# Scale sums at first use, seven banks for the MLP's products, three single-block groups at each end, a last norm by halves and square sums on GpSimd

## The chip, the cores and the metric

The program runs on one core of a Trainium2 chip, in one launch. The metric is its device time in microseconds; of the runs shown the median counts. The profile is of one execution by itself. PE is TensorE, DVE is VectorE, ACT is ScalarE, POOL is GpSimd, and SP is the engine that issues most transfers.

## The reference

One decoder layer on 2048 tokens of width 1024, in float32 throughout; h is the normed x of the line above:

```python
mem_n = rmsnorm(mem, mem_norm_g)                    # 256 memory tokens
q, k, v, g, u = split(rmsnorm(x) @ w_in)            # 512 columns each
y_ret = silu(g) * head_rmsnorm(retention(rope(q), rope(k), v))   # 4 heads
y_pool = pool_mixer(u, pool_w) * pool_scale         # windows 2, 4, 8, 16
x = x + concat(y_ret, y_pool) @ w_out
x = x + softmax((h @ wq) @ (mem_n @ wk).T / 16) @ (mem_n @ wv) @ wo   # 4 heads
a = h @ w_up                                        # 5632 columns
c = conv_w[0]*a[t-2] + conv_w[1]*a[t-1] + conv_w[2]*a[t] + conv_b
x = x + (silu(c[:, :2816]) * c[:, 2816:]) @ w_down
return rmsnorm(x, final_norm_g)
```

## The kernel before

The activations lie transposed: a tile holds 128 features by 512 tokens. The 2048 tokens are two blocks (b = 0, 1) of 1024, each with two halves (s = 0, 1). Every large product is a form with seven multiplications (i = 0 to 6) in place of eight: the weight of a pair of output tiles is four quarters, of which seven sums are made (`make(i)`), and the tokens are made into seven sums likewise. Each sum is cut into a high and a low fp16 part by `cut` (L274 on ACT for the high part, L241 or L232 on DVE for the low one), and `passes` multiplies high by high, high by low and low by high (L289, L290, L291). So one of the seven products of one block is 12 matmuls of 128x128 by 128x512 for an up group, and a group of one block is 84.

Before a weight is cut it is scaled by a power of two. `fetch` loads its four quarters, ACT squares each (L250), and `power` adds the four sums on DVE (L260), adds them over the partitions by a one-column matmul on PE (L264, into a bank of the ring called side) and makes the scale from the exponent (L236, L238). The cut needs that scale.

What sets the order: the program is written in one line of Python, in which `step` mixes side work (generators, put in with `beside(gen, rate)`) into the products at a rate per product, and a scheduler then orders the instructions of each engine, earlier code first where several are ready. The order within an engine is fixed when the kernel runs. PSUM has eight banks, handed out in rings: for the MLP six are for the products (mm) and two for the small matmuls (side).

The stages:

- 0 to about 150 us: `folded_weights` multiplies the memory into the attention's weights and W_o, `x_block` squares the tokens of block 0 and norms them, and the rope tables are made. `stats` adds squares over the features by matmuls against a column of ones (L315), DVE makes the reciprocal root in eleven small operations, and `spread` puts the result on all partitions: a diagonal matrix by DVE (L232), then a matmul against ones (L328).
- 150 to about 1213: input projections, retention, pooling, output projection and cross-attention.
- 1213 to 2070: the up products. `Up` groups f = 0 to 21 give a pair of gate and value tiles, with convolution (`conv`) on ACT (L1217), DVE and, for sums, POOL. The first EARLY groups and the last LATE run for block 0 alone and then, with their cut weights read back from WUd, for block 1 alone; the others run for both blocks at once. While the first round runs, `mlp_tokens(1)` norms, sums and cuts the tokens of block 1. While the fourth runs, `down_weights` cuts the down weights and writes them to WDd.
- 2070 to 2531: the down products (`Down`), three parts of four groups for each block, with weights read from WDd (L1127) and tokens read from Gd. After the last part of block 0 its final norm runs beside the products of block 1.
- 2531 to 2554: the final norm of block 1, over both halves, and its outputs (L1354, L1361).

`run` makes weight sums ahead of the product that needs them, up to seven products ahead (AHEAD). `squares` (ACT squares, another engine adds) takes the engine of the add as its argument. The names in the listings: mm, aux and side are PSUM banks; G and FD are the pools of SBUF tiles; rn and rnm hold norms, sm small results, sb sums, scl_t scales, taps the scaled convolution weights.

## Time and the profile before

| | us |
|---|---|
| three runs | 2557.42, 2563.1, 2565.51 |
| median | 2563.1 |
| the profiled execution | 2555.96 |
| its span on the core | 2554.2 |
| PE busy | 2386.9 (93%) |
| DVE busy | 1689.4 (66%) |
| ACT busy | 1221.1 (48%) |
| POOL busy | 567.7 (22%) |

A row of the windows gives, for a stretch of the span, its length, then the busy time and the number of instructions of PE, of PE's weight loads, of DVE, ACT and POOL, then the clock granted to PE, the share of the DMA engines and GB/s. A row of waits reads: engine, what it was to write and its line, what released it; then the waiting time in all, how often, and the longest. A row of the timeline starts with the time from the span's start and the duration; behind the shapes stands how many instructions it groups and, in brackets, how long the engine had been idle and what ended that. A busy PE is not a PE at its peak, because the matmuls overlap: their starts are what counts.

### The profile page before, as it was taken

How to read it: one execution, taken by the hardware profiler on the slowest of the kernel's cores; microseconds unless marked ns; L12 is line 12 of the kernel's file. 1: busy time of each engine (PE TensorE's matmuls, PEld its weight loads, DVE VectorE, ACT ScalarE, POOL GpSimd, SP SyncE). 2: the span in 40 equal slices, each digit the busy share in tenths (PEclk: the TensorE clock that was granted, in tenths of full speed). 3: DMA queues.
4: the chain of work that ended last, by engine and by line, in shares of the span. 5: the costliest groups of instructions: out<-in, count | busy, mean ns of one | idle time of the engine just before them, and what ended most of it. 6: DMA issues, size and time to landing. Idle time of an engine off the chain costs nothing. (4 is left out here: it accounts for less than half of the span.)

```text
span 2554.2 us, 32142 instructions
## 1 busy us (share of the span) xinstructions
PE 2386.9 (93%) x11461; PEld 1178.6 (46%) x11461; DVE 1689.4 (66%) x2852; ACT 1221.1 (48%) x2343; POOL 567.7 (22%) x372
## 2 busy tenths in 40 slices
PE   7799999999999999999799999898999998998997
PEld 7645554465444454444344444343444443444443
DVE  8834888455656462671968786776776786766764
ACT  6763345322643242252467666665765564244322
POOL 0000112011222101312613232432322133323210
PEclk9899999999999999999899999999999999999998
DMA  7671224100443023023233323333323454655751
GB/s 259 201 232 46 75 66 137 37 26 13 158 151 119 34 91 108 33 87 106 86 111 115 101 88 106 116 112 108 120 95 103 161 183 164 206 182 181 239 182 66
DMA packets 177040, 306.67 MB, mean 120 GB/s; under 512 B 18416, under 2 KB 49264, under 8 KB 176880
## 3 DMA queue, kind: packets, MB, share of 16 engines
q1 hardware_dynamic: 175728, 302.52, 35.8%
q8 instruction: 90, 1.47, 0.2%
q10 hardware_dynamic: 1152, 2.10, 0.2%
q14 instruction: 70, 0.57, 0.1%
HBM read 212.53 MB, written 92.01 MB: 119 GB/s over the span
## 5 line engine op out<-in xcount | busy, mean ns | idle before, releaser
L289 PE MATMUL mm<-G 128*128 128x512 f16 x1955 | 744.6, 384 | 57.1 <-DVE FD L232 12.1
L290 PE MATMUL mm<-G 128*128 128x512 f16 x1955 | 749.5, 383 | 2.9 <-DVE G L232 2.5
L291 PE MATMUL mm<-G 128*128 128x512 f16 x1955 | 740.6, 383 | 3.4 <-DVE G L241 2.1
L232 POOL TENSOR_TENSOR G<-G 128x512 f32<-128x512 f32 (+5 forms) x261 | 386.6, 1486 | 1577.8 <-DVE G L241 658.4
L290 PEld LDWEIGHTS <-G 128*128 128x128 f16 x2848 | 280.6, 99 | 368.3 <-issue 53.7
L289 PEld LDWEIGHTS <-G 128*128 128x128 f16 x2848 | 281.1, 99 | 367.0 <-issue 29.0
L291 PEld LDWEIGHTS <-G 128*128 128x128 f16 x2848 | 280.7, 99 | 351.6 <-issue 16.9
L241 DVE SCALAR_TENSOR_TENSOR G<-G,scl_t 128x512 f16<-128x512 f32 (+2 forms) x416 | 343.8, 850 | 141.5 <-ACT G L274 130.3
L274 ACT ACTIVATE G<-G,scl_t 128x512 f16<-128x512 f32 x352 | 244.0, 713 | 307.5 <-POOL G L232 99.6
L241 DVE SCALAR_TENSOR_TENSOR G<-mm,scl_t,G 128x512 f32<-128x512 f32 (+1 forms) x279 | 207.6, 747 | 246.8 <-PE mm L291 228.3
L289 PE MATMUL mm<-FD,G 128*128 128x512 f16 x893 | 340.4, 383 | 3.1 <-ACT G L274 2.3
L291 PE MATMUL mm<-FD,G 128*128 128x512 f16 x893 | 339.8, 381 | 2.5 <-DVE G L241 2.5
L290 PE MATMUL mm<-FD,G 128*128 128x512 f16 x893 | 340.5, 381 | 0.0
L241 DVE SCALAR_TENSOR_TENSOR FD<-FD,taps 128x1024 f32<-128x1024 f32 (+2 forms) x162 | 234.8, 1469 | 37.5 <-ACT FD L1217 36.5
L232 DVE TENSOR_TENSOR G<-G 128x512 f32<-128x512 f32 (+4 forms) x274 | 215.8, 813 | 50.0 <-ACT G L350 17.5
L350 ACT ACTIVATE G<-G 128x512 f32<-128x512 f32 x108 | 67.4, 627 | 204.6 <-DVE G L241 186.3
L250 ACT ACTIVATE G<-G 128x512 f32<-128x512 f32 x136 | 84.9, 625 | 109.1 <-DVE G L241 70.0
L289 PE MATMUL mm<-G,FD 128*128 128x512 f16 x327 | 124.7, 383 | 4.0 <-ACT FD L1191 3.2
L289 PE MATMUL mm<-FD 128*128 128x256 f32 (+2 forms) x313 | 106.9, 344 | 21.3 <-ACT FD L447 7.2
L290 PE MATMUL mm<-G,FD 128*128 128x512 f16 x327 | 124.6, 381 | 0.0
L291 PE MATMUL mm<-G,FD 128*128 128x512 f16 x327 | 124.3, 381 | 0.1
L1217 ACT ACTIVATE FD<-FD,vecs,taps 128x1024 f32<-128x1024 f32 x81 | 99.4, 1235 | 38.1 <-DVE FD L232 37.2
(169 smaller groups left out, 2600.8 us busy)
## 6 DMA issues: line engine op xcount, KB each, us to landing
G<-WDd SPq DMA_DIRECT2D x112, 256.0 KB, 3.5
Gd<-FD SPq DMA_DIRECT2D x41, 512.0 KB, 2.8
G<-xT SPq DMA_DIRECT2D x80, 256.0 KB, 3.3
G<-Gd SPq DMA_DIRECT2D x67, 256.0 KB, 3.6
G<-w_qkgu SPq DMA_DIRECT2D x64, 256.0 KB, 2.9
FD<-w_up SPq DMA_DIRECT2D x45, 256.0 KB, 3.0
G<-w_up SPq DMA_DIRECT2D x43, 256.0 KB, 3.1
G<-WDd SPq DMA_DIRECT2D x56, 192.0 KB, 3.0
```

Of the source, the lines that this page charges most:

```text
L232: return eng.tensor_tensor(out=out, in0=a, in1=b, op=op)
L241: dve.scalar_tensor_tensor(out=out, in0=a, scalar=s, in1=b, op0=op0, op1=op1)
L250: act.activation(junk.f[:, : src.shape[-1]], src, AF.Square, accum_out=col)
L274: act.activation(hi, src, AF.Identity, scale=scale)
L289: pe.matmul(ps, lh, rh, start=start, stop=False, skip_group_check=more)
L290: pe.matmul(ps, lh, rl, start=False, stop=False, skip_group_check=more)
L291: pe.matmul(ps, ll, rh, start=False, stop=stop, skip_group_check=more)
L350: act.activation(q.f, src, AF.Square)
L1217: act.activation(c.f, a[:, at : at + T], AF.Identity, bias=cb[:, f : f + 1], scale=tap[2])
```

## The change

- `Member.fetch` only loads and squares; the scale sum (`power`) moves into `weigh`, which the first `make` of the weight calls.
- The MLP's rings are seven banks for products and one for small matmuls.
- EARLY and LATE go from 2 to 3: three groups at each end run one block at a time, sixteen instead of eighteen run for both. The cut up weights written to WUd and read back go from 28 to 42.
- At the start of the MLP fifteen weight sums are made ahead (FIRST), later up to seven products ahead, and in the down products ten.
- `down_weights` has two more pauses after each fetch and runs at 0.52 steps a product instead of 0.42.
- `spread` is split into `diagonals` and `spread`, with pauses between in `tokens_norm`. The memory norm becomes a generator, and three projections instead of two are begun around its parts.
- The fourteen adds of the token squares of block 0 go from DVE to POOL; half of the evacuations of the W_o product go from DVE to ACT.
- The last norm runs by halves: that of half 1 is written as soon as its last sum exists, that of half 0 after the last product, and then the outputs of the one and of the other. The final norm of block 0 runs at twice its rate.

```diff
-EARLY, LATE = 2, 2
+EARLY, LATE = 3, 3
-AHEAD = 7
+FIRST, AHEAD, AHEAD_DOWN = 14, 7, 10
...
-    def spread(y):
+    def diagonals(y, d=None):
         n = y.shape[1]
-        d = S.take()
-        w = d.f[:, : n * P]
-        tt(dve, w.rearrange("p (a b) -> p a b", a=n), ident.rearrange("p (o b) -> p o b", o=1).to_broadcast([P, n, P]), bcast(y, P), ALU.mult)
-        ps = bank("side")[:, : n * P]
+        d = d or S.take()
+        tt(dve, d.f[:, : n * P].rearrange("p (a b) -> p a b", a=n), ident.rearrange("p (o b) -> p o b", o=1).to_broadcast([P, n, P]), bcast(y, P), ALU.mult)
+        return d, n * P
+    def spread(d):
+        d, n = d
+        ps = bank("side")[:, :n]
+        pe.matmul(ps, ones, d.f[:, :n], start=True, stop=True)
         d.free()
         return ps
...
         yield
+        yield
+        ds = [diagonals(y[:, 4 * s : 4 * s + 4]) for s in range(NS)]
+        yield
+        yield
         for s in range(NS):
-            ps = spread(y[:, 4 * s : 4 * s + 4])
+            ps = spread(ds[s])
             r = S.take()
...
+            yield
             dve.tensor_copy(rn, stats([s_m.f[:, :NMEM]]))
-            act.activation(rm.f[:, :NMEM], spread(rn), AF.Copy)
             s_m.free()
+            d = diagonals(rn)
+            yield
+            act.activation(rm.f[:, :NMEM], spread(d), AF.Copy)
...
-        begun = [project(0, first), project(1)]
-        memory_norm()
+        begun = [project(0, first)]
+        norm = memory_norm()
+        next(norm)
+        begun.append(project(1))
+        next(norm)
+        begun.append(project(2))
+        next(norm, None)
         for n in range(KT):
-            ps = begun[n] if n < 2 else project(n)
+            ps = begun[n] if n < 3 else project(n)
...
                     t, at = S.take(), 4 * h + 2 * mt + nh
-                    ts(dve, t.f, ps, rn[:, mt : mt + 1], ALU.mult)
+                    if nh:
+                        act.activation(t.f, ps, AF.Identity, scale=rn[:, mt : mt + 1])
+                    else:
+                        ts(dve, t.f, ps, rn[:, mt : mt + 1], ALU.mult)
...
-                squares(k, x.f, acc[s].f, dve)
+                squares(k, x.f, acc[s].f, pool if b == 0 else dve)
...
             if self.source is not None:
                 self.raw = True
-                self.up, self.inv = scales[self.key]
                 return
             if self.key not in scales:
-                c = counts(4)
+                self.sums = counts(4)
                 for i, r in enumerate(self.raw.values()):
-                    squared(r.f[:, :w], c[:, i : i + 1])
-                scales[self.key] = power(c, TOP4)
+                    squared(r.f[:, :w], self.sums[:, i : i + 1])
+
+        def weigh(self):
+            if self.key not in scales:
+                scales[self.key] = power(self.sums, TOP4)
             self.up, self.inv = scales[self.key]
         def make(self, i):
             w = self.n * P
+            if i == 0:
+                self.weigh()
...
+            if i == 0 and self.j == KT // 2 - 1 and b + 1 == NB:
+                spare.extend(S.take() for _ in range(4))
             if i in (3, 4, 5):
                 pending.append(lambda: self.out({3: 0, 4: 3, 5: 1}[i]))
+                if i == 5 and self.j == KT // 2 - 1 and b + 1 == NB:
+                    while pending:
+                        pending.pop(0)()
+                    self.half = self.norm_half(1)
             elif i == 6:
                 if self.j == KT // 2 - 1:
                     while pending:
                         pending.pop(0)()
                     self.out(2)
-                    self.norm()
+                    if b + 1 == NB:
+                        late = self.norm_half(0)
+                        self.last_outputs(*self.half)
+                        self.last_outputs(*late)
+                    else:
+                        self.norm()
                 else:
                     pending.append(lambda: self.out(2))
...
-                beside(steps(), 0.5)
-                return
-            y = stats([r.f for r in done])
-            for s in range(NS):
-                ps = spread(y[:, 4 * s : 4 * s + 4])
-                r = S.take()
-                act.activation(r.f, ps, AF.Copy)
+            def steps():
+                yield from tokens_norm(done, rb)
-                    v = Y[b, n // 2, n % 2 * 2 + s].f
-                    if n % 3 == 2:
-                        tt(pool, v, v, r.f, ALU.mult)
-                    else:
-                        tt(dve, v, v, ps, ALU.mult)
-                    (act if n % 2 else sp).dma_start(outputs(n, s), v)
+            beside(steps(), 1.0)
+
+        def norm_half(self, s):
+
+            ps = spread(diagonals(stats([sums[s].f]), spare.pop()))
+            r = spare.pop()
+            act.activation(r.f, ps, AF.Copy)
+            return s, ps, r
+
+        def last_outputs(self, s, ps, r):
+            for n in range(KT):
+                v = Y[self.b, n // 2, n % 2 * 2 + s].f
+                if n % 3 == 2:
+                    tt(pool, v, v, r.f, ALU.mult)
+                else:
+                    tt(dve, v, v, ps, ALU.mult)
+                (act if n % 2 else sp).dma_start(self.outputs(n, s), v)
...
-            while made < len(items) and made <= at + AHEAD:
+            while made < len(items) and made <= max(at + (AHEAD_DOWN if isinstance(m, Down) else AHEAD), FIRST):
...
-    rings.update(mm=[0, 1, 2, 3, 4, 5], side=[6, 7])
+    rings.update(mm=[0, 1, 2, 3, 4, 5, 6], side=[7])
...
                     m.fetch()
-                    yield
+                    for _ in range(3):
+                        yield
                     for i in range(7):
...
-        add([Up(f, [0], sink=kept(f)) for f in late], [0], down_weights(), 0.42)
+        add([Up(f, [0], sink=kept(f)) for f in late], [0], down_weights(), 0.52)
```

Three places in the order of the instructions, each of before and of the change. First DVE in the first rounds of the MLP, where the token sums of block 1 are scaled (L241, by scl_t or a gain) and their low parts cut (L232, G from G), and where the evacuations add a bank to a tile (L232 with mm). Before:

```order
L232 TENSOR_TENSOR G_66<-consts_69,rn_9318 128x512 x2
L232 TENSOR_TENSOR FD_1472<-FD_1472,mm_9383 128x512
L241 SCALAR_TENSOR_TENSOR G_66<-G_66,scl_t_87 128x512 x18
L232 TENSOR_TENSOR G_66<-G_66 128x512
L241 SCALAR_TENSOR_TENSOR G_66<-G_66,scl_t_87 128x512
L232 TENSOR_TENSOR FD_1472<-FD_1472,mm_9343 128x512
L232 TENSOR_TENSOR G_66<-G_66 128x512 x9
L241 SCALAR_TENSOR_TENSOR FD_1472<-FD_1472,taps_9305 128x1023
```

And with the change:

```order
L241 SCALAR_TENSOR_TENSOR G_66<-G_66,scl_t_87 128x512 x9
L232 TENSOR_TENSOR FD_1472<-FD_1472,mm_9538 128x512
L236 TENSOR_SCALAR taps_9925<-vecs_68,scl_t_87 128x6
L232 TENSOR_TENSOR FD_1472<-FD_1472 128x1024
L232 TENSOR_TENSOR G_66<-G_66 128x512 x3
L241 SCALAR_TENSOR_TENSOR G_66<-G_66,scl_t_87 128x512 x9
L232 TENSOR_TENSOR G_66<-G_66 128x512
L232 TENSOR_TENSOR FD_1472<-G_66,FD_1472 128x512
L232 TENSOR_TENSOR G_66<-G_66 128x512
L232 TENSOR_TENSOR FD_1472<-FD_1472,mm_9498 128x512
```

The eighteen scalings in one piece have become two pieces of nine, with an evacuation and a convolution between, and the cuts stand in shorter pieces, with an evacuation after each.

Second DVE in the rounds with both blocks, at two scale sums (L260), the operations that read their matmul (L236 from side), and between them evacuations and convolution. Before, from the first sum on:

```order
L260 TENSOR_REDUCE sb_13618<-sq_86 128x1
L260 TENSOR_REDUCE sb_13723<-sq_86 128x1
L241 SCALAR_TENSOR_TENSOR FD_1472<-FD_1472,scl_t_87 128x512
L232 TENSOR_TENSOR FD_1472<-FD_1472,mm_13544 128x512
L236 TENSOR_SCALAR sm_13617<-side_13620 128x1
L238 TENSOR_SCALAR scl_t_87<-sm_13617 128x1 x2
L236 TENSOR_SCALAR sm_13722<-side_13725 128x1
L232 TENSOR_TENSOR scl_t_87<-scl_t_87 128x1
```

And with the change, from behind the same two sums to the second's reader:

```order
L232 TENSOR_TENSOR FD_1472<-FD_1472,mm_13544 128x512
L236 TENSOR_SCALAR sm_13726<-side_13729 128x1
L238 TENSOR_SCALAR scl_t_87<-sm_13726 128x1 x2
L241 SCALAR_TENSOR_TENSOR FD_1472<-G_66,scl_t_87,FD_1472 128x512
L241 SCALAR_TENSOR_TENSOR FD_1472<-FD_1472,scl_t_87 128x512 x2
L241 SCALAR_TENSOR_TENSOR FD_1472<-G_66,scl_t_87,FD_1472 128x512
L232 TENSOR_TENSOR FD_1472<-FD_1472,mm_13529 128x512
L241 SCALAR_TENSOR_TENSOR FD_1472<-FD_1472,taps_13501 128x1023
L232 TENSOR_TENSOR FD_1472<-FD_1472,mm_13544 128x512
L241 SCALAR_TENSOR_TENSOR FD_1472<-FD_1472,taps_13501 128x1022
L241 SCALAR_TENSOR_TENSOR FD_1472<-FD_1472,taps_13501 128x1024 x2
L236 TENSOR_SCALAR sm_13752<-side_13755 128x1
```

The second sum's reader stood six rows behind its sum before, and stands fifteen behind it now; the sums themselves still stand together. On PE the second sum's matmul stood six rows behind the first's, weight loads counted, and stands 110 behind it now.

Third DVE at the end, where a norm's small operations run on 128 by 8 or by 4 values, G from consts and rn is a diagonal, and the multiplies read side. Before:

```order
L232 TENSOR_TENSOR sm_18395<-rn_18393 128x8
L241 SCALAR_TENSOR_TENSOR sm_18395<-sm_18395,sm_18392 128x8
L241 SCALAR_TENSOR_TENSOR rn_18393<-sm_18395,rn_18393 128x8
L232 TENSOR_TENSOR G_66<-consts_69,rn_18393 128x512 x2
L232 TENSOR_TENSOR G_66<-G_66,side_18407 128x512 x5
L232 TENSOR_TENSOR FD_1472<-FD_1472,side_18407 128x512
L232 TENSOR_TENSOR G_66<-G_66,side_18427 128x512 x4
L232 TENSOR_TENSOR FD_1472<-FD_1472,side_18427 128x512 x2
```

And with the change, from the first half's diagonal on:

```order
L241 SCALAR_TENSOR_TENSOR rn_18417<-sm_18419,rn_18417 128x4
L232 TENSOR_TENSOR G_66<-consts_69,rn_18417 128x512
L232 TENSOR_TENSOR G_66<-G_66,side_18431 128x512 x4
L232 TENSOR_TENSOR FD_1472<-FD_1472,side_18431 128x512 x2
L238 TENSOR_SCALAR sm_18455<-side_18450 128x4
L238 TENSOR_SCALAR rn_18456<-sm_18455 128x4
L232 TENSOR_TENSOR sm_18458<-rn_18456 128x4
```

The multiplies of one half now stand ahead of the small operations of the other, and each half has its own chain of eleven; on PE all of both norms stands behind the last product.

30 lines of the change are left out of this document (12 added, 18 removed).

## The prediction

> **What bounds the kernel now.** I read the windows by stage first, then the waits of TensorE (PE) in each stage, then the timeline at two places.
>
> ```profile
> span 2554.2 us, 32142 instructions
> core 0: us, PE busy (x) PEld busy (x) DVE busy (x) ACT busy (x) POOL busy (x), PEclk, DMA share, GB/s
> 0.00:50.00 50.00, 35.09 (x248) 33.30 (x249) 41.73 (x99) 33.95 (x63) 0.20 (x4) 0.90 0.90 320
> 50.00:100.00 50.00, 36.27 (x256) 34.11 (x255) 49.79 (x100) 30.48 (x65) 0.00 (x0) 0.83 0.36 112
> 100.00:150.00 50.00, 43.54 (x227) 35.95 (x226) 35.90 (x75) 42.07 (x110) 0.00 (x0) 0.96 0.97 313
> 150.00:1200.00 1050.00, 1015.53 (x5028) 512.15 (x5028) 592.79 (x1279) 399.52 (x911) 160.48 (x121) 0.98 0.26 84
> 1300.00:2070.00 770.00, 741.02 (x3418) 332.61 (x3416) 573.41 (x746) 492.46 (x849) 226.63 (x133) 0.99 0.34 114
> 2070.00:2531.00 461.00, 433.49 (x1962) 193.83 (x1961) 305.55 (x426) 173.40 (x259) 125.22 (x82) 0.98 0.53 174
> 2531.00:2554.20 23.20, 5.57 (x19) 3.03 (x18) 11.81 (x27) 2.54 (x4) 4.95 (x4) 0.63 0.49 181
> 1214.00:1250.00 36.00, 30.39 (x129) 14.61 (x130) 33.62 (x60) 17.59 (x31) 17.89 (x10) 0.91 0.30 110
> 1250.00:1324.00 74.00, 56.09 (x232) 23.68 (x232) 61.92 (x65) 42.12 (x76) 32.71 (x19) 0.86 0.32 102
> 1950.00:2000.00 50.00, 50.00 (x235) 22.67 (x233) 34.26 (x38) 29.71 (x52) 13.90 (x8) 1.00 0.36 121
> 2000.00:2050.00 50.00, 50.00 (x236) 22.72 (x235) 32.90 (x57) 24.93 (x38) 8.13 (x6) 1.00 0.46 159
> ```
>
> PE is full almost everywhere from 150 us on. What it costs when nothing stops it:
>
> ```profile
> 1242.66 0.38 PE L289 MATMUL mm<-G 128*128 128x512 f16 x1
> ...
> 1245.04 0.38 PE L291 MATMUL mm<-G 128*128 128x512 f16 x1
> ```
>
> Between these two starts lie eleven matmuls, one every 0.216 us, back to back. The change removes no matmul, so all it can win is what a stage loses over its matmuls times 0.216. That is 110 − 361 × 0.216 = 32 us at the start of the MLP (1214 to 1324), 770 − 3418 × 0.216 = 32 in the up products (the two overlap by 24 us), 461 − 1962 × 0.216 = 37 in the down products, and 150 − 114.9 = 35 idle before 150. The 23.2 behind 2531 are a serial tail. From 150 to 1200 nothing is changed in kind, and I give it 0.
>
> **The parts and their costs.** The waits that carry these losses, line, releaser, total, times, longest, in order of time (before 150, 1200 to 1300, 1300 to 2070, from 2070):
>
> ```profile
> PE mm L291 <- DVE FD L232: 8.9, 3, 6.7
> PE side L328 <- DVE G L232: 5.2, 1, 5.2
> ...
> ACT G L272 <- POOL G L232: 16.7, 7, 7.2
> PE mm L289 <- DVE FD L232: 12.1, 1, 12.1
> ...
> PE side L264 <- DVE sb L260: 11.5, 9, 3.9
> PE mm L289 <- ACT FD L1191: 9.0, 8, 2.9
> DVE sb L260 <- ACT FD L250: 41.0, 15, 4.7
> ...
> PE mm L289 <- DMA G<-WDd: 8.5, 4, 4.3
> PE mm L289 <- ACT G L1271: 7.1, 4, 2.7
> PE side L328 <- DVE G L232: 2.9, 1, 2.9
> ```
>
> **A, the first 150 us.** Fourteen square sums leave VectorE (DVE) for GpSimd (POOL), and eight evacuations leave it for ScalarE:
>
> ```profile
> L232 DVE TENSOR_TENSOR G<-G 128x512 f32<-128x512 f32 x20 | 13.5, 683 | 0.0
> L236 DVE TENSOR_SCALAR G<-mm,rnm 128x512 f32<-128x512 f32 x16 | 11.7, 745 | 0.5 <-PE side L264 0.5
> ```
>
> That is 14 × 0.683 = 9.6 us and 8 × 0.745 = 6.0 us off DVE. The first helps: DVE is busy 49.79 of the 50 us from 50 to 100 while PE idles 13.7. The second lies after 100, where the DMA engines are at 0.97 and DVE has 14 us to spare, so it is worth nothing; ScalarE, with 7.9 us idle there, takes the 6.0. Splitting the memory norm lets PE run a third projection while DVE makes the sums that PE waits for (8.9 + 5.2 = 14.1 us). Best end −13.7, all of PE's idle time in the middle third; worst end +3, if POOL costs DVE more than it takes (second rival). DMA at 0.90 before 50 and 0.97 behind 100 hands part of the gain back, so I take less than half of 14.1: −6.
>
> **B, the start of the MLP.** Here one engine stands in another's way:
>
> ```profile
> 1243.22 25.12 POOL L232 TENSOR_TENSOR G<-G 128x512 f32<-128x512 f32 x12 [10.80 <-DVE G L241]
> 1250.51 14.52 DVE L232 TENSOR_TENSOR G<-G 128x512 f16<-128x512 f32 x9
> ```
>
> Nine DVE subtractions take 1.61 us each, not 0.683, while POOL adds. They cut the second token block, which the second round needs after only two single-block groups (2 × 84 × 0.216 = 36 us). In DVE's order (counted, like all places below, in the listing of instructions) one evacuation stood behind eighteen scalings and the next behind these nine; PE's 12.1 us wait is for DVE there. After, three groups (54 us) stand ahead of the same cuts, which come in nines with evacuations between. The price is two more single-block groups early on DVE: at the rate of the late ones (34.26 + 32.90 = 67 of 100 us, so 12.2 per 18.1 us group) 24 us. DVE then has 33.6 + 61.9 + 24 = 120 us of work where PE has 78 + 36 = 114. If DVE stays as full as before (95.5 of 110, 87%), the stretch takes 138 and loses 24 instead of 32: −8. If DVE could be full, it takes 120 and loses 6: −26. Less overlap with POOL shrinks the 120 as well. I take −12, nearer the first, since DVE's waits on ScalarE and POOL stay. The worst end is the third rival's.
>
> **C, the up products.** The scale sum (DVE L260, PE L264) needs four ScalarE squares, and they need four loads. Before, PE's small matmul stood three to six matmuls behind DVE's sum; after, mostly more than thirteen (13 × 0.216 = 2.8 us). So the nine PE waits at L264 (11.5 us) go. DVE's own 41.0 us wait does not: its sum is still put 12 to 16 matmuls behind the last load. What is late next is an evacuation queued behind DVE's wait, so I count half, −6. The seventh bank takes perhaps a third of the 9.0 at L1191, where PE waits for a bank to be copied out: −3. The side ring falls to one bank, which costs nothing while one sum is in flight at a time. Fourteen more read-backs and write-outs of cut weights go through SP, beside DMA at 0.34; they are covered. C is −9, from 0 (first rival) to −24.
>
> **D, the down products.** Weights are made ten products ahead, not seven (three more, at 12 × 0.216 = 2.6 us each), which covers waits of at most 4.3 us: −6 of the 8.5. The diagonals of the first block's norm stand 5 to 15 matmuls ahead of their spreads, not 2 or 3: −2 of the 2.9. L1271 waits for ScalarE to copy out, and a seventh bank may take some of it; I count none, because the norm's loads and multiplies now come at twice the rate there. More loads ahead queue before the tokens' loads on SP. D is −8, from +3 to −20 (27 us of waits in all, less the quarter that stays in any case).
>
> **E, the tail.**
>
> ```profile
> 2530.56 0.38 PE L291 MATMUL mm<-G 128*128 128x512 f16 x1
> 2530.97 0.75 DVE L241 SCALAR_TENSOR_TENSOR FD<-mm,scl_t,FD 128x512 f32<-128x512 f32 x1 [0.45 <-PE mm L291]
> 2533.17 1.30 PE L315 MATMUL side<-consts,G 128*128 128x1 f32 x8 [1.45 <-DVE G L232]
> 2534.51 0.17 DVE L238 TENSOR_SCALAR sm<-side 128x8 f32<-128x8 f32 x1 [1.40 <-PE side L315]
> 2536.52 0.17 DVE L241 SCALAR_TENSOR_TENSOR rn<-sm,rn 128x8 f32<-128x8 f32 x1
> 2536.72 1.29 DVE L232 TENSOR_TENSOR G<-consts,rn 128x512 f32<-128x512 f32 x2
> 2537.46 3.55 PE L328 MATMUL side<-G,ones 128*128 128x512 f32 x4 [2.99 <-DVE G L232]
> 2540.20 3.08 DVE L232 TENSOR_TENSOR G<-G,side 128x512 f32<-128x512 f32 x5 [2.19 <-ACT G L1354]
> 2546.19 1.28 DVE L232 TENSOR_TENSOR FD<-FD,side 128x512 f32<-128x512 f32 x2
> ```
>
> Both half norms stand behind the last product on PE. With one side bank the second half's sums cannot start before the first half's last DVE multiply has read it, so the chains run one after the other. A half chain is 0.65 for four sums (half of 1.30), 2.2 for eleven small operations, 0.65 for a diagonal, 1.8 for a spread (half of 3.55), and 6 × 0.62 for the multiplies (3.08 over five): 9.0. The first runs from the end of the last matmul, 2530.56 + 0.38 (T), while the other half's last square is still being made; two give T + 18 and some hand-overs, 18.9. Before, the last multiply ended at 2547.47, T + 16.5. Half of the outputs leave earlier, which I put at 0.5 back. E is +2, from −1 to +4.
>
> **Sum.** −6 −12 −9 −8 +2 = −33. The profiled execution ran 2555.96 with a span of 2554.2, 7 under the median of 2563.1. From its time the sum gives 2523; from the median, which I take, 2530. About 0.3%, 7.7 us, is what a measurement of this kernel can tell from no change.
>
> **Rivals.** First, the change doesn't do what it says: the sums hardly move on DVE (12 to 16 matmuls behind the loads in both), so the 41.0 us stays, PE's wait only changes its name, and C is 0: 2539. Against it stands the PE order, 3 to 6 matmuls turned to 13.
>
> Second, the squares on POOL are no gain. Beside POOL's adds of 25.12 / 12 = 2.09 us, DVE took 1.61 instead of 0.683, so each POOL add cost it up to 2.09 × 0.93 / 1.61 = 1.2 us. Fourteen cost up to 17 where 9.6 are saved: A is 9 worse at +3, and the time 2539. For it speaks that DVE's work in the first 100 us is mostly of the two-SBUF-input kind; against it, that the tokens come with the DMA-bound loads before 50, where DVE has 8 us idle. The Trainium skill, "SBUF — State Buffer", section "Who interferes with whom", says that a DVE instruction with two SBUF inputs contends with a GpSimd instruction that reads SBUF, under an exclusive lock. The 1.61 against 0.683 agrees; by the rule alone each of the fourteen adds would hold DVE up, A would be +3 and the time 2539.
>
> Third, it ends slower: single-block groups are DVE-bound at the front. Each of the two early ones that stand beside the token cuts lost 32 / 2 = 16 us. If a third one loses 16 too (DVE 120 against PE 114, fed worse than now) and a third late pair, which now shares with faster weight making, another 16, B is +16 and C +7: 2574. It decides from where DVE's work passes PE's. Against it: the late groups run with PE at 50.00 of 50 and DVE at 67%.
>
> **Chances.** Forecast 0.45, with a range of its own of 2518 to 2541; first rival 0.13, second 0.12; better than forecast, with B and D near their good ends (−26 and −20, so −59: 2504), 0.1; parts that cancel, 2555 to 2571, 0.1; third rival or another loss of its size 0.1. I go to 2504 below and to 2556 above. Faster 0.81, same 0.1, slower 0.09.
>
> **What would show it.** In the profile after: PE's waits at L264 under 3 us between 1300 and 2070 while DVE's before L260 stay near 40; the wait of 12.1 gone and less than 24 us lost in the first 145 us of the MLP; WDd waits under 3; the tail 25 us; PE's idle time before 150 near 29. Wrong would make it a new PE wait on DVE in the early single groups, on the single side bank, or on tokens' loads (Gd) queued behind weights.

## The result, and the profile after

| | before | after |
|---|---|---|
| median of 4 runs each on one chip, us | 2560.26 | 2590.85 |
| lowest to highest | 2557.42 to 2565.51 | 2587.47 to 2594.42 |
| the profiled execution | 2555.96 | 2592.76 |
| its span | 2554.2 | 2590.8 |

The ratio is 1.0117, with a 95% interval of 1.0092 to 1.0142: the change makes the kernel 1.2% slower. The forecast was 2530, its range ended at 2556 and held at 0.81 that it would be faster. It was wrong in sign.

The windows of the changed kernel, by the same stages (the MLP begins about 25 us later, near 1239; the columns are those of the page before):

```profile
span 2590.8 us, 32222 instructions
0.00:50.00 50.00, 34.08 (x240) 32.44 (x240) 44.31 (x78) 31.35 (x61) 20.00 (x18) 0.90 0.84 300
50.00:100.00 50.00, 41.40 (x305) 39.04 (x305) 48.08 (x97) 32.30 (x72) 0.00 (x0) 0.90 0.44 131
100.00:150.00 50.00, 35.92 (x162) 27.34 (x161) 33.38 (x69) 43.57 (x113) 0.00 (x0) 0.82 1.03 350
1238.00:1376.00 138.00, 113.75 (x497) 49.40 (x496) 105.77 (x151) 73.29 (x127) 53.46 (x30) 0.91 0.35 117
2098.00:2561.80 463.80, 432.02 (x1972) 193.65 (x1969) 305.08 (x429) 172.58 (x256) 117.30 (x81) 0.99 0.54 178
```

From 50 to 100, where DVE is busy nearly all the time, PE is busy 41.40 us instead of 36.27: that is the gain that was forecast. From 100 to 150 it is busy 35.92 instead of 43.54, at a clock of 0.82 instead of 0.96: the gain is gone, and more. PE's idle time before 150 is 38.6 us, where the forecast had 29 and before had 35.

Line numbers are each kernel's own. Stages end at other times in every kernel, so the kernels are set against each other at equal work. PE's matmuls, each at its duration at full clock, come to 2311 us in every kernel. The table says how many us a kernel is behind (+) or ahead of (−) the profiled execution of before when PE has done so much of them. The columns answer to these times of before: 126, 152, 285, 375, 485, 1207, 1342, 2083, 2521 and the end. So 80 to 100 is the time when block 0 is prepared, 220 to 400 belongs to the retention stage, 1100 to 1200 is the start of the MLP, 1200 to 1900 the up products, 1900 to 2300 the down products.

```
                80    100    220    300    400   1100   1200   1900   2300    end
after         -9.7   +4.7   +7.5  +18.2  +21.7  +24.5  +22.4  +28.9  +31.4  +36.6
e1_start      -9.9   +5.1   +5.5  +12.2  +17.6  +21.0  +19.4  +14.8  +16.9  +16.6
e18_squares  -10.5   +6.6   +7.8   +6.9   +4.6   +7.1   +8.0   +6.9  +14.4  +14.3
e4_memnorm    +1.9   +1.1   -0.2   -1.3   -2.4   -1.0   -7.3   -8.0   -4.0   -3.8
e2_vw         -0.9   +3.2   +2.0   +0.3   -1.5   +0.7   +0.9   +2.1   +8.7   +9.0
e14_notok     -9.5   +5.5   +5.9  +11.7  +10.5  +11.9   +5.6   +8.0  +10.2  +10.2
e3_tokens     -8.1   -1.5   -2.2   +1.5  +18.2  +22.9  +15.4   +7.9  +11.9  +11.5
e13_x0        -8.3   -2.6   -3.1   -4.2   +7.0  +11.7   +5.7   +0.1   -0.1   -0.9
e5_rate       -7.9   -1.8   -2.8  +18.5  +30.4  +36.5  +34.3  +33.1  +35.1  +34.3
e9_x1        -10.4   +3.3   +5.4  +11.4  +21.3  +24.4  +23.8  +39.8  +35.8  +41.3
e12_ahead    -10.1   +3.1   +5.7  +13.9  +20.4  +24.1  +25.5  +40.4  +28.8  +34.6
e11_early2    -9.5   +6.3   +9.2  +17.6  +20.4  +24.4  +21.3  +22.7  +19.3  +25.0
e10_groups2   -9.8   +5.7   +6.7  +15.9  +20.4  +24.1  +20.8  +24.6  +16.2  +21.4
e6_weigh      +2.6   +1.4   +1.8   +1.5   -0.2   +1.3   +1.6   -4.4   -4.4   -3.8
e7_rings      -1.7   -2.7   -3.4   -5.3   -7.0   -7.4  -11.0  -14.4  -18.5  -17.3
e15_good      -1.0   -1.1   -2.1   -3.9   -3.5   -3.0   -6.5  -15.8  -19.3  -18.1
e17_good5     -1.7   -2.3   -3.3   -5.1   -7.7   -7.4  -11.0  -21.5  -24.9  -24.1
e16_good_mem  -0.5   -1.2   -0.9   -2.2   -2.8   -1.5   -1.8   -6.6  -12.5  -11.5
e8_halves     -0.2   -0.4   -1.4   -0.8   -3.4   -2.5   -2.3   -3.8   +1.4   +2.7
```

How far a single execution can be trusted: e6, e7, e8, e15 and e17 are before's program up to the MLP, and at 1100 they stand from −7.4 to +1.3. In the MLP, kernels with the MLP code of before (e1 to e5, e13, e14, e18; in e1, e3, e5 and e13 with the pauses in its token norm) move between −11.8 and +8.0 from 1100 to 2300. Two of them, e2 and e18, run the MLP's instructions on PE, DVE and ACT in the very order of before, by their traces, and still fall behind by 8.0 and 7.3 there. So differences of some 8 us between two executions are not told apart. The column at 100 falls into a wait, and moves by 1 to 3 us with the place in it. e9 to e12 ran on a chip on which before took 2567.58, 12 us more than the execution that the table compares with; part of their last columns may be that.

### The profile page after: what moved, and what is told of

Read it like the earlier page. It is cut to its first block, busy times and chain, and to the rows that moved or that the text cites. A ratio compares the mean times of both kernels' runs of the same rounds, so it can differ in the third digit from the quotient of the medians.

```text
span 2590.8 us, 32222 instructions
## 1 busy us (share of the span) xinstructions
PE 2401.6 (93%) x11461; PEld 1181.7 (46%) x11461; DVE 1689.5 (65%) x2851; ACT 1222.9 (47%) x2355; POOL 581.0 (22%) x386
## 5 line engine op out<-in xcount | busy, mean ns | idle before, releaser
L289 PE MATMUL mm<-G 128*128 128x512 f16 x2000 | 763.9, 386 | 60.4 <-ACT G L274 13.2
L232 POOL TENSOR_TENSOR G<-G 128x512 f32<-128x512 f32 (+4 forms) x286 | 420.9, 1477 | 1727.3 <-DVE G L241 724.6
L290 PE MATMUL mm<-G 128*128 128x512 f16 x2000 | 769.2, 385 | 0.0
L291 PE MATMUL mm<-G 128*128 128x512 f16 x2000 | 761.3, 384 | 4.4 <-DVE G L241 4.4
L289 PEld LDWEIGHTS <-G 128*128 128x128 f16 x2916 | 288.9, 99 | 402.6 <-issue 34.3
L241 DVE SCALAR_TENSOR_TENSOR G<-G,scl_t 128x512 f16<-128x512 f32 (+2 forms) x442 | 374.1, 867 | 148.8 <-ACT G L274 139.4
L290 PEld LDWEIGHTS <-G 128*128 128x128 f16 x2916 | 288.3, 99 | 388.5 <-issue 71.3
L291 PEld LDWEIGHTS <-G 128*128 128x128 f16 x2916 | 288.3, 99 | 361.3 <-issue 18.4
L274 ACT ACTIVATE G<-G,scl_t 128x512 f16<-128x512 f32 (+1 forms) x378 | 261.8, 712 | 305.5 <-POOL G L232 78.4
L289 PE MATMUL mm<-FD,G 128*128 128x512 f16 x916 | 350.2, 384 | 21.7 <-DMA G<-WUd 13.4
L291 PE MATMUL mm<-FD,G 128*128 128x512 f16 x916 | 349.9, 382 | 2.8 <-DVE G L241 2.8
L290 PE MATMUL mm<-FD,G 128*128 128x512 f16 x916 | 350.3, 382 | 0.0
L241 DVE SCALAR_TENSOR_TENSOR G<-mm,scl_t,G 128x512 f32<-128x512 f32 (+1 forms) x267 | 198.2, 747 | 228.2 <-PE mm L291 215.2
L241 DVE SCALAR_TENSOR_TENSOR FD<-FD,taps 128x1024 f32<-128x1024 f32 (+2 forms) x156 | 219.2, 1419 | 35.1 <-ACT FD L1239 33.7
L232 DVE TENSOR_TENSOR G<-G 128x512 f32<-128x512 f32 (+5 forms) x258 | 195.8, 785 | 64.5 <-ACT G L357 18.8
L250 ACT ACTIVATE G<-G 128x512 f32<-128x512 f32 x148 | 92.9, 632 | 132.3 <-DVE G L241 63.4
L289 PE MATMUL mm<-FD 128*128 128x256 f32 (+2 forms) x324 | 110.3, 345 | 27.3 <-ACT FD L454 8.4
L291 PE MATMUL mm<-FD 128*128 128x256 f32 (+2 forms) x324 | 108.5, 339 | 1.4 <-DVE FD L232 1.4
L290 PE MATMUL mm<-FD 128*128 128x256 f32 (+2 forms) x324 | 109.4, 339 | 0.4 <-DVE FD L232 0.2
L232 DVE TENSOR_TENSOR FD<-FD,mm 128x512 f32<-128x512 f32 x122 | 82.7, 681 | 35.7 <-PE mm L291 18.9
```

What stands on the lines that cost most here:

```text
L232: return eng.tensor_tensor(out=out, in0=a, in1=b, op=op)
L241: dve.scalar_tensor_tensor(out=out, in0=a, scalar=s, in1=b, op0=op0, op1=op1)
L250: act.activation(junk.f[:, : src.shape[-1]], src, AF.Square, accum_out=col)
L274: act.activation(hi, src, AF.Identity, scale=scale)
L289: pe.matmul(ps, lh, rh, start=start, stop=False, skip_group_check=more)
L290: pe.matmul(ps, lh, rl, start=False, stop=False, skip_group_check=more)
```

## The experiments

Every kernel below ran once beside a run of before on its chip, apart from e17, which was timed in five rounds.

### What of the start costs

**e1_start**: before with all edits outside the MLP, as the diff of the change has them (the squares on POOL, the memory norm in parts, the W_o evacuations on ACT, the pauses in `tokens_norm`). 2572.59 against 2556.16.

> The kernel before with the change's edits of the first 150 us and of tokens_norm alone (memory norm as a generator, diagonals apart from spreads, token squares on GpSimd, half of the W_o evacuations on ScalarE); the MLP and the last norm as before. The changed kernel's PE is 9.7 us ahead of before when it has done 80 us of matmuls (each counted at its time at full clock), 4.7 behind at 100, 7.5 behind at 220 and 24.5 behind at 1100. Theory: these edits alone make that lag, so the same four numbers come again within 1 us, and the whole is 20 to 28 us over before. Rival: the lag comes from the MLP's edits by the scheduler's order; then it is under 5 us at 1100.

It is 16.6 us behind at the end and 21.0 when the MLP begins. At 80 and 100 the changed kernel's numbers come again within 1 us, at 220 and 1100 within 2.0 and 3.5. Most of the loss of the whole change lies ahead of the MLP.

**e2_vw**: before with only the evacuations moved. 2565.04 against 2556.16.

```diff
-                    ts(dve, t.f, ps, rn[:, mt : mt + 1], ALU.mult)
+                    if nh:
+                        act.activation(t.f, ps, AF.Identity, scale=rn[:, mt : mt + 1])
+                    else:
+                        ts(dve, t.f, ps, rn[:, mt : mt + 1], ALU.mult)
```

> The kernel before with only half of the W_o evacuations moved to ScalarE. Theory: ScalarE's queue holds the evacuation behind casts that wait for loads, so PE waits for banks: between 80 and 100 us of matmuls it falls back by 6 to 14 us, and about as much of it is left at 1100. Rival: ScalarE has room, no lag over 2 us anywhere, and the 13.6 us come from the loads, which the earlier work meets sooner.

No gain by 80 (−0.9), 4.1 lost from there to 100, where 6 to 14 were expected, and +0.7 at 1100. Of its 9 us 6.6 come in the down products, where none of its code is; that is within what single executions differ by.

**e3_tokens**: before with only the split of `spread` and the pauses in `tokens_norm`. 2567.5 against 2556.16.

```diff
+        yield
+        ds = [diagonals(y[:, 4 * s : 4 * s + 4]) for s in range(NS)]
+        yield
+        yield
         for s in range(NS):
-            ps = spread(y[:, 4 * s : 4 * s + 4])
+            ps = spread(ds[s])
```

> The kernel before with only tokens_norm changed: diagonals apart from spreads and three more pauses. Theory: the pauses shift the norm of the second token block among the retention's small chains, which costs the 17 us that the changed kernel loses between 220 and 340 us of matmuls; so +12 to +18 there and under 3 before 200. Rival: these 17 come from the memory norm or the squares, and this kernel loses under 5 there.

The pauses bring 8 us by 80, keep little of it at 220 (−2.2), and lose 16.7 from 300 to 400, in a stage that the prediction had put at 0.

**e4_memnorm**: before with only the memory norm in parts and three projections begun. 2552.35 against 2556.16.

```diff
-        begun = [project(0, first), project(1)]
-        memory_norm()
+        begun = [project(0, first)]
+        norm = memory_norm()
+        next(norm)
+        begun.append(project(1))
+        next(norm)
+        begun.append(project(2))
+        next(norm, None)
```

> The kernel before with only the memory norm changed: its three parts between three begun projections. Theory: it gives the 9.7 us that the changed kernel is ahead at 80 us of matmuls (so -5 to -10 here), most of it lost again by 100 to the loads, which fill the DMA engines from 100 us on. Rival: the squares gave the 9.7, and this kernel is within 3 us of before at 80.

At 80 it is 1.9 behind, as the rival had it: it gives nothing there. So the 14.1 us of waits that the prediction hung on it were not to be had in this way.

**e18_squares**: before with only the square sums of block 0 moved. 2570.22, against a median of 2559.73.

```diff
-                squares(k, x.f, acc[s].f, dve)
+                squares(k, x.f, acc[s].f, pool if b == 0 else dve)
```

> The kernel before with only the token squares' adds moved to GpSimd. The fourteenth experiment, which has them and no pauses, lost 15 us between 80 and 100 us of matmuls and 6 between 220 and 260; the memory norm alone and the evacuations alone lost 4 at most and 0 there. Theory: the squares take the 6 between 220 and 260 by the order that follows, and 4 or more between 80 and 100, by an earlier start into the loads. Rival: only the three together do it; then this kernel is within 3 us of before at 400. The prediction's rival of a blocked DVE would show before 60: behind there by 3 or more, where the fourteenth is 4 ahead.

This one line gives the −10.5 at 80 and the +6.6 at 100. From 80 to 100 it loses 17.1. What happens there, in the timeline of its PE and then of its DVE (L236 is the evacuation of a W_o product):

```profile
128.03 0.50 PE L289 MATMUL mm<-FD 128*128 128x512 f32 x1 [0.64 <-DVE G L236]
131.89 0.77 PE L289 MATMUL mm<-FD 128*128 128x512 f32 x1 [2.20 <-DVE G L236]
...
147.72 0.79 PE L289 MATMUL mm<-FD 128*128 128x512 f32 x1 [10.97 <-DVE G L236]
```

```profile
146.92 0.75 DVE L236 TENSOR_SCALAR G<-mm,rnm 128x512 f32<-128x512 f32 x1 [7.74 <-DMA rope_d<-G]
```

PE arrives earlier in a stretch where the DMA engines are at 1.01 of full. There an evacuation stands in DVE's order behind a tile that is still being written out to DRAM; PE runs out of banks and waits 10.97 us, and a matmul behind a wait takes 0.77 to 0.79 us there, where one took 0.50 before.

**e14_notok**: before with the edits of e2, e4 and e18, without the pauses. 2566.18 against 2554.49.

> The kernel before with the memory norm's generator, the token squares on GpSimd and half of the W_o evacuations on ScalarE, and tokens_norm as before. If tokens_norm is the cause of the lag between 220 and 400 us of matmuls, it is under 3 there, and the lag at 100 tells what the squares and evacuations cost: 3 to 8. If squares or evacuations are the cause, 8 or more are lost between 220 and 400.

It loses 5.8 from 220 to 300, which none of its parts loses alone (e2, e4, e18), and nothing from 300 to 400, where e3 loses its 16.7. Over both that is 4.6, between the two cases that were set out.

**e5_rate**: e3 with the norm of block 1 stepped faster. 2590.32 against 2554.6.

```diff
-            beside(x_block(1, X[1]), 0.7)
+            beside(x_block(1, X[1]), 0.77)
```

> The kernel of the third experiment (tokens_norm's pauses alone, which fell 18 us behind between 330 and 360 us of matmuls) with x_block of the second token block at 0.77 steps a product instead of 0.7, so that its 38 steps need as many products as 35 did. Theory: the three more pauses push the end of that norm past the end of the first block's projections, where it is drained in one lump and holds back the loads of the second block's weights; then the lag at 360 goes from +18 to within 3 of before, the gain of 8 at 80 stays, and the whole ends 5 to 15 us under before. Rival: the loss comes from the order of the small operations as such; then +10 or more stays at 360.

My theory was that the pauses make `x_block(1)` finish late. A higher rate should have mended that; the lag at 400 went from +18.2 to +30.4 instead.

**e13_x0**: e3 without the pauses in `x_block(1)`. 2555.05 against 2554.49.

```diff
-        yield from tokens_norm(acc, rb)
+        yield from tokens_norm(acc, rb, pauses=b == 0)
```

> The kernel before with tokens_norm's new pauses in every norm but that of the second token block. In the changed kernel with the same exception (ninth experiment) 20 us of lag stayed at 400 us of matmuls. Theory: any of the pauses ahead of the retention makes the scheduler order that stage anew, and that order loses: 10 or more lost between 220 and 400 here. Rival: with the second block's norm where it was, these pauses alone are harmless (under 5 between 220 and 400), and the squares or the evacuations on ScalarE make the ninth's lag.

The same lines of code are kept away from block 1, and from 300 to 400 it still loses 11.2.

**e9_x1**: the changed kernel without the pauses in `x_block(1)`, by the same edit. 2597.45 against 2567.58.

> The changed kernel, in which the norm of the second token block (x_block for b = 1, run beside the retention of the first) keeps the old pauses; every other norm has the new ones. Theory: the 18 us that the changed kernel loses between 220 and 360 us of matmuls come from where these pauses put that norm among the retention's operations, and go: the lag at 400 is under 10 instead of 21.7, and the whole about 2575. Rival: the earlier start of the whole stage makes the loss; then 20 us of lag stay at 400.

At 400 and 1100 it stands where the changed kernel stands (+21.3 and +24.4). The theory fell a second and a third time.

What all of them have in common is shown by the stretch from 220 to 1100. The nine kernels with the pauses (after, e1, e3, e5, e9 to e13) lose from 14.8 to 39.3 there; the ten runs without them (e2, e4, e6 to e8, e14 to e18; e15 and e17 are one kernel) lie between −4.1 and +6.0, four with the split of `spread` among them. So the edit of `tokens_norm` is a cause: three more pauses, and both diagonals made ahead of both spreads, which no run takes apart. The loss does not need it in block 1. Nor is it the whole loss: e14, which is e1 without this edit, loses 6.0 there and e1 15.5, so that the edit accounts for some 10 of the changed kernel's 17.

The traces also give the order in which the instructions ran. The changed kernel, e1, e10, e11 and e12 have one order of PE, DVE and ACT in this stretch, and lose from 15.2 to 18.4; e2, e6, e7, e8, e15 and e17 have that of before on DVE and ACT, and lie between −4.1 and −0.5. So the loss goes with the order. In the changed kernel some 110 of 1111 DVE instructions and 80 of 806 on ACT have changed places. A new order alone is not yet a loss: e4 has 79 and 37 in other places and stands at −0.8.

And there is a place where the edit costs. Between 320 and 370 us of work, while new projection weights (w_qkgu, w_v) are loaded, the nine kernels with it lose from 4.6 to 18.4, and the ten runs without lie between −4.7 and +0.3. The longest waits of PE there, in e3, e13 and the changed kernel (rows of each; e5 has one like e13's, of 8.6):

```profile
PE side L264 <- DVE sb L260: 7.3, 1, 7.3
```

```profile
PE mm L289 <- ACT FD L274: 8.7, 1, 8.7
```

```profile
PE aux L889 <- DVE G L241: 3.4, 2, 2.6
PE mm L289 <- ACT G L274: 3.1, 1, 3.1
```

They are not one wait, but mostly for the scale or the cut of a weight. In e3 the trace shows what stands behind it: SP's queue waits for a tile that DVE frees only at 447.1, and the loads behind it come in one lump. SP's wait from 425 to 462, then the windows:

```profile
SPq L295 <- DVE G L232: 10.9, 1, 10.9
```

```profile
440.00:450.00 10.00, 4.44 (x12) 1.60 (x12) 8.32 (x9) 3.71 (x12) 6.97 (x5) 0.79 0.17 46
450.00:460.00 10.00, 3.68 (x11) 1.41 (x11) 8.13 (x16) 8.90 (x15) 0.00 (x0) 0.53 1.02 334
```

Before, PE was busy 19.40 of these 20 us. For the other kernels it stays open what their waits go back to, and for all of them on which of the moved instructions the loss hangs.

### The MLP, one part at a time

**e6_weigh**: before with the scale sums at first use. 2552.14 against 2554.6.

```diff
-                scales[self.key] = power(c, TOP4)
+        def weigh(self):
+            if self.key not in scales:
+                scales[self.key] = power(self.sums, TOP4)
...
+            if i == 0:
+                self.weigh()
```

> The kernel before with only the scale sum moved to first use. The prediction: PE's waits at the sum's matmul go from 11.5 us to under 3 between 1300 and 2070, and the up products gain 3 to 6. Rival: the waits on PE only change their name, DVE still waits about 41 us at the sum, and the kernel stays within 4 us of before from 1150 to 1900 us of matmuls.

From 1200 to 1900 it gains 6.0, the −6 of the prediction, but in one execution, and less than one can tell. PE's waits at L264 from 1300 to 2070 fall from 11.5 to 6.8, not to under 3, and its wait for the gate's evacuation rises from 9.0 to 10.8; DVE's wait stays, at 45.4. So part of the waits did change their name.

**e7_rings**: before with seven product banks. 2538.62 against 2554.6.

```diff
-    rings.update(mm=[0, 1, 2, 3, 4, 5], side=[6, 7])
+    rings.update(mm=[0, 1, 2, 3, 4, 5, 6], side=[7])
```

> The kernel before with only the MLP's banks changed: seven for products, one for small matmuls. The prediction: PE's waits for ScalarE's copies of a bank in the up products fall from 13 us by about 3, and nothing else moves. Rival: the single side bank costs, by the scale sums and by the last norm's two spreads, which must share it: +3 or more, of which 2 to 4 in the tail.

It gains 3.4 from 1200 to 1900 (predicted 3), but also 3.6 at the start of the MLP and 4.1 in the down products, where the prediction had put none. Of its 17.3 us 7.4 lie ahead of the MLP, where it is before's program. And the waits do not show the reason that was given: from 1300 to 2070 L1191 stands at 8.8 (before 9.0), and L264 has risen from 11.5 to 15.1, as the rival had it for the scale sums. What fell are the waits at the gate's other copy (L1189, from 2.8 to none) and for DVE's additions (from 3.6 to 0.7).

```profile
PE side L264 <- DVE sb L260: 15.1, 9, 4.1
PE mm L289 <- ACT FD L1191: 8.8, 5, 3.2
```

**e15_good, e17_good5**: these two edits together and nothing else; the same kernel under two names. e15 took 2537.89 against 2554.49, and gained 16.3 from 1100 to 2300.

> The kernel before with the two edits that gained by themselves: scale sums at first use (6 us in the MLP) and seven banks for products (11 us there). Theory: they take away different waits, so the MLP gains 12 to 18 against before from 1100 to 2300 us of matmuls, and the whole ends near 2540. Rival: each gain was one draw of the scheduler's order; then the two together gain under 8.

> The kernel of the fifteenth experiment once more, timed in rounds: scale sums at first use and seven banks, nothing else of the change. One look gave 2537.89 beside 2554.49. If the gain is of the MLP, the ratio is 0.993 to 0.996; if the look was lucky in the first 400 us of matmuls, where kernels with one order differ by up to 9 us, it is 0.997 or more.

In five rounds it took 2536.29 (2531.84 to 2543.71, 6 runs) against 2559.73 (2551.51 to 2565.42, 11 runs): a ratio of 0.9917, from 0.9899 to 0.9935, somewhat better than expected. It beats both kernels. The execution in the table is the fastest of the six, and 7.4 of its 24.1 us lie ahead of the MLP. PE's waits from 1300 to 2060 in it:

```profile
PE mm L289 <- ACT FD L1199: 8.4, 7, 1.9
PE mm L289 <- ACT FD L1195: 5.5, 3, 3.0
PE side L264 <- DVE sb L260: 5.0, 5, 2.4
```

L264 falls from 11.5 to 5.0.

**e16_good_mem**: the same with e4's edit, the memory norm in parts. 2544.49 against 2554.49.

> The same two edits and the memory norm's generator, which alone ended 4 us under before. If gains add, 2535; if every edit ahead of the MLP draws its order anew, anything from 2530 to 2560.

The memory norm adds nothing here either.

**e8_halves**: before with the last norm by halves (the change's edits of `evac`, `norm`, `norm_half` and `last_outputs`) and its two side banks. 2558.63 against 2554.6.

> The kernel before with only the last norm by halves, and two side banks as before. The time from the start of the last product's last matmul to the end was 23.6 us before and is 29.4 with the whole change, where the prediction had 25.6. Theory: the one side bank makes the two halves run one after the other; with two banks they interleave and the tail is within 2 us of 23.6. Rival: the two chains of small operations cost the 6 us by themselves, and the tail is 27 or more here too.

From the start of the last product's last matmul to the end of the span it takes 24.9 us, before 23.6, after 29.4. So the six us come from the single side bank; with two banks the halves cost 1.3 us and gain nothing.

### The changed kernel with a part undone

**e10_groups2**: two groups at each end, and the pace of `down_weights` as before. 2577.91 against 2567.58.

```diff
-EARLY, LATE = 3, 3
+EARLY, LATE = 2, 2
...
-                    for _ in range(3):
-                        yield
+                    yield
...
-        add([Up(f, [0], sink=kept(f)) for f in late], [0], down_weights(), 0.52)
+        add([Up(f, [0], sink=kept(f)) for f in late], [0], down_weights(), 0.42)
```

> The changed kernel with two single-block groups at each end instead of three, and the down weights made at the pace of before. Alone, the moved scale sums gained 6 us and the seven banks 11 in the MLP, yet the whole change loses 7 there. Theory: the third groups cost the difference, so that from 1100 to 2300 us of matmuls this kernel gains 10 to 20 against before and ends near 2570. Rival: the edits are not additive, or making ahead costs it; then it still loses 0 or more there.

**e11_early2**: two groups in front, three at the end. 2581.2 against 2567.58.

```diff
-EARLY, LATE = 3, 3
+EARLY, LATE = 2, 3
```

> The changed kernel with two single-block groups at the front and three at the end. If the front's third group is what costs (its cut weights come back from HBM 13.4 us late), the MLP to 1400 us of matmuls is 10 us or more better than in the changed kernel. If the end's third group costs, nothing changes before 1800 and the down products stay as slow.

**e12_ahead**: weight sums made seven ahead throughout, as before. 2590.64 against 2567.58.

```diff
-            while made < len(items) and made <= max(at + (AHEAD_DOWN if isinstance(m, Down) else AHEAD), FIRST):
+            while made < len(items) and made <= at + AHEAD:
```

> The changed kernel with weight sums made seven products ahead everywhere, as before. The prediction gave making ten ahead 6 us in the down products, 1900 to 2300; so 6 are lost there here. Rival: fifteen ahead at the start and ten later only take tiles that other loads wait for; then this kernel is level or better, and the 13.4 us wait for read-back weights is shorter.

From 1100 to 2300 the three kernels with a third group in front lose (after 6.9, e9 11.4, e12 4.7), the two without it gain (e11 5.1, e10 7.9, where 10 to 20 were expected). The means are 14 us apart. That the third group in front costs about so much is likely, but five executions, of which any two may differ by 8 us with one order, do not show it, and the place fits only in part: by 1400, where 10 us were expected, e11 is 3 us better than the changed kernel. The third group at the end shows no price (e11 and e10 are 3 apart). Of making ahead nothing is shown either: from 1900 to 2300, where e12 was to lose 6, it gains 11.6.

## Why the prediction was wrong, point by point

The 36.6 us by which the spans differ, as the table divides them:

| | predicted | measured |
|---|---|---|
| A, to 100 us of work | −6 | +4.7 |
| from there to 1100 | 0 | +19.8 |
| B, 1100 to 1200 | −12 | −2.1 |
| C, 1200 to 1900 | −9 | +6.5 |
| D, 1900 to 2300 | −8 | +2.5 |
| E, behind 2300 | +2 | +5.2 |

All terms but E are about 10 us or more off. **"From 150 to 1200 nothing is changed in kind, and I give it 0": the step that failed.** About half of the loss is there. The prediction treated the order of an unedited stage as given. But one scheduler orders the whole program, and the edit of `tokens_norm` puts the norm's instructions among other products: some 110 of 1111 DVE instructions and 80 of 806 on ACT changed places between 220 and 1100, and kernels with that order lose 15.2 to 18.4 there. Some 10 of it is that edit's; the other 6 came with the edits of the start (e14). From 250 to 450 DVE is busy about 40 of 50 us, which leaves little room; that this is why a worse order costs so much there is argued, not shown. The profile of before could not give the sign. The listing of the order, of which three places stand ahead of the prediction, tells whether a stage is reordered; the term should then have had a range of some 20 us.

**A: right that the squares put PE ahead, wrong about why and what it is worth.** "The first helps": the squares alone put PE 10.5 us ahead at 80 (e18). "DMA at 0.90 before 50 and 0.97 behind 100 hands part of the gain back, so I take less than half": it hands back all, and 5 more. The waits of PE from 90 to 170 in the changed kernel:

```profile
PE mm L289 <- ACT G L609: 5.8, 1, 5.8
PE mm L289 <- ACT FD L454: 4.7, 2, 4.2
```

L609 is the evacuation that went to ACT. "ScalarE, with 7.9 us idle there, takes the 6.0" left out what is queued in front of it:

```profile
142.61 0.63 ACT L250 ACTIVATE G<-G 128x512 f32<-128x512 f32 x1 [0.57 <-DMA WPd<-G]
...
143.28 0.69 ACT L609 ACTIVATE G<-mm,rnm 128x512 f32<-128x512 f32 x1
```

```profile
144.01 0.80 PE L289 MATMUL mm<-FD 128*128 128x512 f32 x1 [5.79 <-ACT G L609]
```

From 139.50 on, five squares (L250) stand ahead of the evacuation for which PE waits; the last of them waits until a write to WPd has landed.

The second rival, that the squares on POOL hold DVE up, was right about DVE. Groups of the first 50 us, before and after:

```profile
L232 DVE TENSOR_TENSOR FD<-G,FD 128x512 fp32r<-128x512 f32 x30 | 20.1, 685 | 2.5 <-ACT FD L447 2.3
L232 DVE TENSOR_TENSOR sm<-rn 128x2 f32<-128x2 f32 x3 | 0.5, 153 | 0.0
```

```profile
L232 DVE TENSOR_TENSOR FD<-G,FD 128x512 fp32r<-128x512 f32 x28 | 22.1, 820 | 0.9 <-ACT FD L454 0.6
L232 DVE TENSOR_TENSOR sm<-rn 128x2 f32<-128x2 f32 x3 | 2.5, 845 | 0.1
L232 POOL TENSOR_TENSOR G<-G 128x512 f32<-128x512 f32 x14 | 19.8, 1441 | 23.5 <-ACT G L357 20.9 <-issue 2.6
```

28 × (820 − 685) ns is 3.8 us, another 7 of 256 columns go from 416 to 945 ns, 3.7 us, and the small operations of the memory norm (153 to 845 ns above) and a few more add some 6. That is more than the 9.6 us that DVE was spared: it is busy 92.4 of the first 100 us, and was 91.5 before. PE was ahead at 80 all the same, not because DVE had less to do, but because other things came first: when PE had done 80 us of work, DVE had run 201 instructions in e18 and 234 before, and only 14 of the missing ones had gone to POOL. A ended at +4.7, near the +3 of this rival, but the loss came behind 80, in the stretch full of transfers.

**B: the wait went, and another took its place.** The 12.1 us for DVE are gone. In the changed kernel PE waits 13.4 us for a weight read back from WUd, and the 138 us from 1238 on lose 31 (497 matmuls of 0.216), where under 24 of the first 145 was forecast. PE at the place, then SP's queue, then what SP waits for from 1285 to 1350:

```profile
1319.92 0.38 PE L291 MATMUL mm<-G 128*128 128x512 f16 x1
1333.73 0.61 PE L289 MATMUL mm<-FD,G 128*128 128x512 f16 x1 [13.43 <-DMA G<-WUd]
```

```profile
1316.40 9.63 SPq L1149 DMA_DIRECT2D G<-WUd  x4
...
1330.93 2.68 SPq L1149 DMA_DIRECT2D G<-WUd  x4
```

```profile
SPq L1163 <- DVE G L241: 23.4, 3, 10.3
SPq L1149 <- PE mm L291: 16.6, 3, 11.9
SPq L1149 <- DVE G L232: 14.8, 7, 6.1
```

"Fourteen more read-backs and write-outs of cut weights go through SP, beside DMA at 0.34; they are covered" counted the engines that move the bytes, not the queue that issues them. In that queue a read-back waits until its SBUF tile is free (L1149 on PE or DVE), and a write-out (L1163) waits for the cut of the weight; all behind them wait too. And the tiles are late because of DVE. While PE waits, DVE is busy all the time, with the cuts of the second token block, 1.26 us each (6.29 / 5) beside POOL's work; the read-back of 1330.93 was issued when the cut of 1330.18 was done, and landed at 1333.7:

```profile
1320.00:1334.00 14.00, 0.57 (x3) 0.13 (x2) 14.00 (x14) 6.37 (x12) 7.29 (x4) 0.61 0.33 98
```

```profile
1320.57 6.29 DVE L232 TENSOR_TENSOR G<-G 128x512 f16<-128x512 f32 x5
...
1330.18 0.68 DVE L232 TENSOR_TENSOR G<-G 128x512 f16<-128x512 f32 x1
```

So the third rival named the right place and the right engine, though not the way by which PE is held: DVE's work on the token cuts passes PE's, and PE meets it through SP's queue. An average hides this: over the 138 us DVE is busy 105.77, 77%, less than the 87% before. The price of 16 for a third group in front is near the 14 that lie between the means of the five runs, which alone do not show it. All of these kernels have long waits here (e12 9.7 for a cut and 9.8 for a scale sum, e9 15.0 and 10.1; with two groups in front, e10 and e11, the longest is 9.9).

The Trainium skill, "TensorE: Matmul & The Clock Gate", section "HAM oscillation — how this bites in real kernels", holds that an idle gap above some 3.4 us throttles PE to half its clock. The row of 1333.73 agrees: behind 13.43 us of idling a matmul takes 0.61 where it took 0.38, and the next ones start 0.42 us apart instead of 0.22. The row of e18 at 131.89 had 0.77 behind 2.20 us already, with shorter gaps ahead of it, so one gap need not reach the page's figure. The prediction's waits are idle time alone. Over the whole span PE loses 25.8 us more than before by having no matmul to run, and 14.5 more by matmuls that take longer than at full clock (both summed over all its matmuls). The two keep no fixed ratio: in e17 it is 7.1 and 13.1 less than before.

**C: near for its two parts in sum, lost in the whole.** Scale sums and the seventh bank by themselves gain 9.3 (e15) and 10.5 (e17) from 1200 to 1900, where 9 was forecast; e7 and e6 show that the waits did not fall as the two terms had it, so part of this agreement is luck. In the changed kernel the same waits, from 1324 to 2098 behind the one of B, are:

```profile
...
PE mm L289 <- ACT FD L1217: 11.7, 7, 3.1
PE side L264 <- DVE sb L260: 9.7, 6, 2.5
PE mm L289 <- ACT FD L1213: 7.7, 5, 2.7
...
DVE sb L260 <- ACT FD L250: 38.0, 14, 4.6
```

L264 keeps 9.7 of 11.5, where under 3 was forecast (5.0 in e17); DVE's wait stays near 40, as forecast. PE's wait for a gate's evacuation on ACT falls from 9.0 to 7.7 (L1213, before L1191), and that for a value's rises from 1.1 to 11.7 (L1217, before L1195). The e17 kernel has the same two at 5.5 (L1195) and 8.4 (L1199): the gate's wait falls by more than the third that was forecast, and more than that is then waited for at the value. The first rival, that PE's wait only changes its name, is borne out in part: in e6 4.7 us went from L264, and 1.8 came at the gate. In the changed kernel C loses, 15.5 us from the forecast; the third group in front is the likely cause, not a shown one.

**D: ten ahead do not reach the wait, and others changed their engine.** From 2098 to 2561:

```profile
PE mm L289 <- DVE G L241: 10.7, 8, 3.3
PE mm L289 <- DMA G<-WDd: 7.4, 4, 2.6
PE mm L289 <- DVE FD L241: 7.1, 4, 2.7
...
PE mm L289 <- ACT G L1293: 2.4, 2, 1.7
```

Of the same stretch before, the rows on DVE:

```profile
PE mm L289 <- DVE G L241: 3.2, 2, 2.0
...
PE mm L289 <- DVE FD L241: 2.7, 3, 1.5
```

WDd falls only from 8.5 to 7.4. The evacuation on ACT falls from 7.1 to 2.4, and the one on DVE (L241) rises from 5.9 to 17.8. The term of 6 for making ten ahead is the one that failed here: WDd was to fall under 3, and e12, without it, does no worse.

**E: the chain was sized too short.** The serial halves were foreseen, at 18.9 us from T to the last multiply's end. PE and DVE there:

```profile
2561.43 0.38 PE L291 MATMUL mm<-G 128*128 128x512 f16 x1
2564.04 1.05 PE L315 MATMUL side<-consts,G 128*128 128x1 f32 x8 [2.23 <-DVE G L232]
2568.14 2.04 PE L331 MATMUL side<-G,ones 128*128 128x512 f32 x2 [3.04 <-DVE G L232]
2574.58 1.87 PE L315 MATMUL side<-consts,G 128*128 128x1 f32 x8 [4.40 <-DVE FD L232]
2579.49 2.05 PE L331 MATMUL side<-G,ones 128*128 128x512 f32 x2 [3.04 <-DVE G L232]
```

```profile
2570.85 2.48 DVE L232 TENSOR_TENSOR G<-G,side 128x512 f32<-128x512 f32 x4 [2.86 <-ACT G L1384]
2573.24 1.28 DVE L232 TENSOR_TENSOR FD<-FD,side 128x512 f32<-128x512 f32 x2
2584.60 1.28 DVE L232 TENSOR_TENSOR FD<-FD,side 128x512 f32<-128x512 f32 x2
```

The first half takes 10.5 (2564.04 to 2574.52), not 9.0. Its sums take 1.05, not 0.65: the 1.30 that the prediction halved were one half's already, as the eight L315 of one half show. Its spread takes 2.04, not 1.8, and 0.7 go by until ACT's copy lets DVE multiply, for which the sum had no term. The second half takes 11.3. And the first does not start at T (2561.81), beside the last square of the other, but at 2564.04, when DVE has added that square. The last multiply ends at T + 24.1. With two side banks the whole tail was 24.9 (e8).

## What to carry to other kernels

Where one scheduler orders the whole program, an edit need not be local: compare the order of the later stages with the one before (here the evacuations left it as it was and the pauses did not), give each stage that is reordered a range, and test the edits one at a time. Two of these edits were worth 0.8%, and the bundle lost 1.2%. When work is moved onto an engine or a queue with idle time, read what stands ahead of it there and what that waits for, not the busy share of a long stretch. A faster stage is worth only what the next stage can take: see whether the stretch behind it is at the limit of its transfers.
